# Gate table stored from ScalarE's queue, two more raw buffers and more gather steps in the U stage, a last V group of 4, and a halved id sum

## The chip, the cores and the metric

The kernel runs on one core of a Trainium2 chip. The metric is device time in microseconds (us), the median of several executions. PE is TensorE, DVE is VectorE, ACT is ScalarE, POOL is GpSimd, SP is the engine that issues most DMAs.

## The reference

One decoder layer over 16 meta tokens and 512 sequence tokens of width 2048: RMSNorm, differential attention and an mLSTM side by side, an output projection, and a PEER feed-forward. All in fp32. The change lies in the PEER part:

```
q = (ht @ w_q).reshape(T, 8, 2, 128)
s = einsum('thpd,hpnd->thpn', q, sub_keys)
s1, i1 = top_k(s[:, :, 0], 16);  s2, i2 = top_k(s[:, :, 1], 16)
cand_s = s1[..., :, None] + s2[..., None, :]
cand_i = i1[..., :, None] * 128 + i2[..., None, :]
best_s, best_pos = top_k(cand_s, 16)
idx = take_along_axis(cand_i, best_pos)          # 8 x 16 experts of 16384 for each token
gate = softmax(best_s)
act = gelu(einsum('td,tkd->tk', hb, u[idx]))
y = einsum('tk,tkd->td', gate * act, v[idx])
```

## The kernel before

**Dense and gathered tokens.** For ND = 352 tokens the kernel computes the PEER layer densely: all 16384 rows of `u` against these tokens (the U stage, 128 chunks of 128 experts), then all rows of `v` (the V stage), with a gate table that is zero where an expert was not chosen. The other 160 tokens are served by gathering: 128 of them in jobs "d" and "a", 32 (folded into 32 jobs "D" and "A") beside them. That makes NJ = 320 gather jobs, each an indirect DMA of 128 rows x 2048 floats (1.049 MB) issued by POOL at L836, and one DVE instruction that uses it (L844 with rows of `u`, L857 with rows of `v`). Three row buffers `ug` exist, so POOL is up to three gathers ahead of DVE. `run(n)` emits gather steps until n have been done.

**Order.** PE and DVE work in the order in which the program is written (a manual schedule), POOL too from the gate table on. ACT's and SP's queues are ordered by the scheduler of the framework, and each is served first in, first out.

**The routing stage (about 970 to 1160 us).** `step(n)` for n = 2 to 15 multiplies by `w_q` on PE while `bgstep()` runs the top-k in a pipeline of tasks: DVE max/index instructions, POOL's candidate grids `cd` (L935 to L939), the one-hot product `oh` on POOL (L969, 50 candidates x 16) and the DVE sum over the candidates `ids` (L974). A step does one `bgstep()`, every fourth step two, so 18 in these 14 steps; the other 16 fall among the first 31 U chunks.

**The U stage (about 1160 to 2262 us).** `u_chunk(c)` loads a chunk's weights in two halves of 128x1024 floats (512 KB each, `load_half` on SP's queue, three buffers `raw`), splits each into a high part (`hid`, ACT, L79) and a low part (`lod`, DVE, L80), which go into five buffers of each kind, and multiplies: 16 k-tiles x 3 matmuls of 352 columns (L89 to L91). The result goes through Gelu (`at`, L889) to the DRAM table `Ad` (L890, ACT's queue, 176 KB).

From chunk 32 on, the gate table is built beside it, four tokens at a time, 88 sets. `ebuild(q)` makes one-hot tiles on DVE (L1076 to L1079) and a scaled copy `ea` on ACT (L1081). The tiles `e` and `eg` are laid out as [128 keys, 4 tokens], so that one token's column has a step of four bf16 elements; `ea` is laid out densely. `gbuild(q)` is 12 matmuls of 128 columns (L1092), an ACT copy into the staging tile `stg` (L1093) and, every eighth set, the store of 2 MB to the DRAM table `Gd` from SP's queue (L1095). `stg` has one buffer.

`pace(c)` spreads the gather steps: from the 15 steps done before chunk 32 to JU = 150 at chunk 127. The last UTAIL = 6 chunks also hold the preparation of the first V group: loads of `Gd` and `Ad` (`p_load`, ACT's queue), the product `tm` (L1135) and its split into `ah` and `al` (L1145, L1146).

**The V stage (about 2262 to 3317 us).** Expert rows are handled in groups, GROUPS = [8] + [16] x 7 + [8] (sum 128). All groups but the last produce the transposed output (L1275 to L1277, 352 columns), 24 matmuls an item, an item being a 512 KB piece of `v` loaded as `rawv`; at the end of a group half, eight PSUM banks are added to `yT` on DVE (L1287). The last group (L1304 to L1306, 512 columns) runs token by token and ends with the final norm and the stores. Of six consecutive `rawv` loads three use the pool of the U stage, three a pool `vr` that lies on memory which the U stage holds until its end. In V, `run` spreads the remaining steps over all items but three of the transposed groups.

Of the kernel before, what the change touches and what calls it, by code (L numbers as in the profile page):

```python
# [8 lines left out]
F = mybir.dt.float32  # L9
R = mybir.dt.float32r  # L10
BF = mybir.dt.bfloat16
# [30 lines left out]
NQ = 128 // NB  # L42
SB = 128 // NQ
ND = S - 128 - NB
GROUPS = [8] + [16] * 7 + [8]
NJ = 2 * (128 + SB)
JU = 150
AR = 20
AR1 = 8

# [10 lines left out]
def body(tc, I, out):  # L61
    nc = tc.nc
    top = ExitStack()
    with top:
# [3 lines left out]
        dp = top.enter_context(tc.tile_pool(name="dp", bufs=1, space=DRAM))  # L68

        def load_half(src, name, rawp=None):  # L70
            raw = (rawp or wp).tile([128, 8, 128], F, name="raw" + name, tag="raw", bufs=3)
            nc.sync.dma_start(raw, src.rearrange("p (k c) -> p k c", k=8))
            return raw

        def split_half(src, name, raw=None, eng=nc.vector):
            raw = raw or load_half(src, name)
            hi = wp.tile([128, 8, 128], R, name="hi" + name, tag="whi")
            lo = wp.tile([128, 8, 128], R, name="lo" + name, tag="wlo")
            nc.scalar.copy(hi, raw)  # L79
            eng.tensor_tensor(lo, raw, hi.bitcast(F), op=OP.subtract)  # L80
            return hi, lo

        def split_tile(src, name):
            return [split_half(src[b], f"{name}_{b}") for b in range(2)]

        def mm3(ps, w, k, xh, xl, cs):
            hi, lo = w[k // 8]
# [578 lines left out]
def rest(tc, I, out, L):  # L666
# [150 lines left out]
    up = sU.enter_context(tc.tile_pool(name="up", bufs=1))  # L817
    iota = up.tile([128, 128], F, name="iota")
    nc.scalar.dma_start(iota, I["c_iota"])
    iota4 = up.tile([128, 128, 4], BF, name="iota4")  # L820
    nc.vector.tensor_copy(iota4, bcast(iota, 4))
    n1T = up.tile([128, ND], BF, name="n1T")
    n2T = up.tile([128, ND], BF, name="n2T")
    gp = up.tile([128, 3, ND], BF, name="gp")
# [46 lines left out]
    sp = [I["wq"][i] for i in range(16)] + [I["u"][c] for c in range(NK)]  # L871
    w[2] = split_tile(sp[2], "d2")

    def step(n, mid=None):
        if n + 1 < len(sp):
            w[n + 1] = split_tile(sp[n + 1], f"d{n + 1}")
        ps = pmu.tile([128, 512], F, name="pu", tag="pu")
        nn = S if n < 16 else ND
        for k in range(KD):
            mm3(ps[:, :nn], w[n], k, h2h, h2l, slice(0, nn))  # L880
            if k == 7 and mid:
                mid()
        w.pop(n)
        return ps
# [7 lines left out]
    with tc.tile_pool(name="tk", bufs=1) as tk, \  # L892
# [34 lines left out]
        def head_tasks(h, b):  # L927
            st = {}
            cs = slice(16 * h, 16 * h + 16)

            def grid(dst, lo, hi):
                o = 0
                for i in range(5):
                    n = 16 // (i + 1)
                    nc.gpsimd.tensor_tensor(dst[:, o:o + n], lo[:, :n], bcast(hi[:, i], n), op=OP.add)  # L935
                    o += n
                nc.gpsimd.tensor_tensor(dst[:, o:o + 6].rearrange("p (a c) -> p a c", c=2), bcast_mid(lo[:, :2], 3),
                                        bcast(hi[:, 5:8], 2), op=OP.add)
                nc.gpsimd.tensor_tensor(dst[:, o + 6:o + 14], hi[:, 8:16], bcast(lo[:, 0], 8), op=OP.add)  # L939

            bv = (gsel if b == 3 else gs[:, b])[:, cs]

            def t1():
                sv = tk.tile([128, 2, 16], F, name="sv", tag="sv", bufs=3)
                si = tk.tile([128, 2, 16], U32, name="si", tag="si", bufs=3)
                st["sv"], st["si"] = sv, si
                return [(sv[:, p, :], si[:, p, :], hd[h, p][:, b, :]) for p in range(2)]

            def t1b():
                sv, si = st["sv"], st["si"]  # L950
                cd = tk.tile([128, 2, NCAND], F, name="cd", tag="cd", bufs=4)
                sif = tk.tile([128, 2, 16], F, name="sif", tag="sif", bufs=3)
                nc.scalar.activation(sif[:, 0, :], si[:, 0, :], AF.Copy, scale=128.0)
                nc.scalar.copy(sif[:, 1, :], si[:, 1, :])
                grid(cd[:, 0, :], sv[:, 1, :], sv[:, 0, :])
                grid(cd[:, 1, :], sif[:, 1, :], sif[:, 0, :])
                st["cd"] = cd

            def t2():
                st["bp"] = tk.tile([128, 16], U32, name="bp", tag="bp", bufs=3)  # L960
                return [(bv, st["bp"], st["cd"][:, 0, :])]

            def t2b():
                bpb = tk.tile([128, 16], BF, name="bpb", tag="bpb", bufs=3)
                nc.vector.tensor_copy(bpb, st["bp"])
                eq = tk.tile([128, NCAND, 16], BF, name="eqb", tag="eqb", bufs=2)
                nc.vector.tensor_tensor(eq, iom, bcast_mid(bpb, NCAND), op=OP.is_equal)
                oh = tk.tile([128, NCAND, 16], F, name="oh", tag="oh", bufs=2)
                nc.gpsimd.tensor_tensor(oh, eq, bcast(st["cd"][:, 1, :], 16), op=OP.mult)  # L969
                st["oh"] = oh  # L970

            def t3():
                oh = st["oh"]
                nc.vector.tensor_reduce(ids[:, b, cs], oh.rearrange("p c k -> p k c"), axis=AX.X, op=OP.add)  # L974
                if b == 3:
                    nc.vector.tensor_copy(idx[:, cs], ids[:, 3, cs])
                    routed.append(h)
            return t1, t1b, t2, t2b, t3
# [84 lines left out]

    with tc.tile_pool(name="gk", bufs=1, reuse_waits="tile") as gk, \
            tc.tile_pool(name="psg", bufs=2, space=PSUM) as psg, \
            tc.manual_schedule(engines={mybir.EngineType.Pool}):
        stg = {}

        ge = {}

        def ebuild(q):
            t0 = 4 * q
            e = gk.tile([128, 2, 128, 4], BF, name="e", tag="e", bufs=2)
            eg = gk.tile([128, 2, 128, 4], BF, name="eg", tag="eg", bufs=2)
            ea = gk.tile([128, 4, 128], BF, name="ea", tag="ea", bufs=2)
            nc.vector.tensor_tensor(e[:, 0], iota4, bcast_mid(n1T[:, t0:t0 + 4], 128), op=OP.is_equal)  # L1076
            nc.vector.tensor_tensor(e[:, 1], iota4, bcast_mid(n2T[:, t0:t0 + 4], 128), op=OP.is_equal)
            for i in range(2):
                nc.vector.tensor_tensor(eg[:, i], e[:, 1], bcast_mid(gp[:, 1 + i, t0:t0 + 4], 128), op=OP.mult)  # L1079
            for j in range(4):  # L1080
                nc.scalar.activation(ea[:, j, :], e[:, 1, :, j], AF.Copy, scale=g0[:, t0 + j:t0 + j + 1])  # L1081
            ge[q] = e[:, 0], [ea.rearrange("p j n -> p n j"), eg[:, 0], eg[:, 1]]

        def gbuild(q):
            tg, r = divmod(4 * q, TG)
            if r == 0:
                stg[tg] = gk.tile([128, NK, TG], F, name="stg", tag="stg")
            e1, eg = ge.pop(q)
            pg = psg.tile([128, 4, 128], F, name="pg", tag="pg")
            for j in range(4):  # L1090
                for i in range(3):
                    nc.tensor.matmul(pg[:, j, :], e1[:, :, j], eg[i][:, :, j], start=(i == 0), stop=(i == 2))  # L1092
            nc.scalar.copy(stg[tg][:, :, r:r + 4], pg.rearrange("p j n -> p n j"))  # L1093
            if r + 4 == TG:
                nc.sync.dma_start(Gd[tg, :, 0:NK, :], stg[tg])  # L1095

        gr2.append(sG.enter_context(tc.tile_pool(name="gr2", bufs=1, side="right")))
        acc["D"] = gr2[0].tile([128, D], F, name="h2nB", tag="h2nB")
        for q in range(NQ):
            nc.scalar.dma_start(acc["D"][NB * q:NB * q + NB], hB)  # L1100
        ng, n0, c0 = 0, nj[1], ci
        ebuild(0)

        def pace(c):
            run(n0 + int((c + 1 - c0) * (JU - n0) / (NK - c0)))

        for c in range(ci, NK - UTAIL):
            u_chunk(c)
            while ng < min(ND // 4, (c + 1 - ci) * (ND // 4) / (NK - 12 - ci)):
                gbuild(ng)  # L1110
                ng += 1
                if ng < ND // 4:
                    ebuild(ng)
            pace(c)
    sU.close()

    with ExitStack() as sV:
# [40 lines left out]
        def vload(i):  # L1158
            if i < len(vord):
                g, dc, pr, c = vord[i]  # L1160
                vraw[i] = load_half(I["v"][g0s[g] // 2 + pr, dc if g == NG - 1 else 2 * dc + c], "v",
                                    None if i % 6 < 3 and i < nlast - 4 else vr[0])

        def vsplit(i):
            if i < len(vord):
# [27 lines left out]
        for c in range(NK - UTAIL, NK):  # L1193
            if c == NK - 1:
                for i in range(VLA):
                    vload(i)
                    vsplit(i)
            u_chunk(c)
            for _ in range(-(-len(pro) // (NK - c))):
                f, q = pro.pop(0)  # L1200
                f(q)
            pace(c)
        assert not pro
        sQ.close()
        sD.close()
# [258 lines left out]
```

## Time and profile before

| | |
|---|---|
| median of 3 executions | 3329.25 us (3327.45 to 3330.25) |
| the profiled execution | 3331.74 us |
| its span, first to last instruction | 3330.0 us |
| PE busy | 3264.0 us (98%) |
| DVE, ACT, POOL busy | 2320.2, 1325.5, 943.9 us |
| mean granted TensorE clock | 0.992 of full speed |
| moved by DMA | 815.47 MB, mean 245 GB/s |

Busy is the union of an engine's instructions. Matmuls overlap in the profile (a 352-column matmul is shown with some 325 ns but the next starts 160 ns after it), so PE's share alone does not say how close PE is to its rate; the number of matmuls in a stretch does.

### The profile page before, as it was taken

What the parts mean: (1) busy time and instruction counts of PE and PEld (TensorE: products, weight loads), DVE (VectorE), ACT (ScalarE), POOL (GpSimd) and SP (SyncE); (2) the same over time, 40 slices, a digit from 0 to 9 for tenths busy, and PEclk for the clock granted to TensorE, in tenths of its full rate; (3) what the DMA queues carried; (4) which work ended last, traced back from release to release, by engine and by line L of the source; (5) the groups of instructions that cost most, each with busy time, mean ns of one, the idle gap of its engine ahead of it and who ended that gap; (6) DMA issues with size and microseconds to landing.
All of it is one profiled execution on the core that took longest, in us unless ns stands there. A gap on an engine that the chain in (4) does not pass through costs nothing.

```text
span 3330.0 us, 51020 instructions
## 1 busy us (share of the span) xinstructions
PE 3264.0 (98%) x20126; PEld 3067.1 (92%) x20126; DVE 2320.2 (70%) x3504; ACT 1325.5 (40%) x2219; POOL 943.9 (28%) x942
## 2 busy tenths in 40 slices
PE   8999999999999999999999999997999999999998
PEld 7889898888887899999999999997999999999996
DVE  7444444444367788787877778767888888888973
ACT  5444444453252233444544544433333333333323
POOL 2011111110015566423332233322323323323312
PEclk8999999999999999999999999998999999999999
DMA  4222121123353266588888978999999999999972
GB/s 154 70 70 77 64 77 64 64 70 115 127 186 136 87 221 226 206 323 316 332 343 325 361 297 348 354 362 337 377 354 375 372 365 370 375 364 372 379 279 101
DMA packets 230162, 815.47 MB, mean 245 GB/s; under 512 B 21697, under 2 KB 85697, under 8 KB 186529
## 3 DMA queue, kind: packets, MB, share of 16 engines
q1 hardware_dynamic: 105488, 400.72, 33.3%
q0 software_dynamic: 46080, 335.56, 25.7%
q10 hardware_dynamic: 78352, 75.92, 6.8%
q8 instruction: 158, 2.59, 0.3%
q14 instruction: 84, 0.68, 0.1%
HBM read 757.33 MB, written 54.79 MB: 244 GB/s over the span
## 4 chain that ended last, share of the span: by engine, by line
PE 85%; DVE 8%; DMA 2%; issue 2%; ACT 1%; POOL 1%; ACTq 0%; SPq 0%; POOLq 0%; DVEq 0%
PE pu L89 10%; PE pu L90 10%; PE pu L91 10%; PE py L1275 8%; PE py L1277 8%; PE py L1276 8%; PE ps L89 5%; PE ps L91 5%; PE ps L90 5%; PE pg L1092 3%; PE po L742 2%; PE po L740 2%; PE po L741 2%; DVE y L857 1%; DVE lov L80 1%
## 5 line engine op out<-in xcount | busy, mean ns | idle before, releaser
L89 PE MATMUL pu<-hh,hid 128*128 128x352 f32 (+1 forms) x2272 | 759.8, 334 | 0.2 <-ACT at L889 0.2
L90 PE MATMUL pu<-hh,lod 128*128 128x352 f32 (+1 forms) x2272 | 751.3, 331 | 3.1 <-DVE lod L80 3.1
L91 PE MATMUL pu<-hl,hid 128*128 128x352 f32 (+1 forms) x2272 | 750.2, 330 | 0.0
L1275 PE MATMUL py<-ah,hiv 128*128 128x352 f32 x1920 | 627.0, 327 | 20.5 <-ACT hiv L79 9.5
L1276 PE MATMUL py<-ah,lov 128*128 128x352 f32 x1920 | 623.4, 325 | 8.8 <-DVE lov L80 8.8
L1277 PE MATMUL py<-al,hiv 128*128 128x352 f32 x1920 | 625.5, 326 | 0.0
L79 ACT CAST hiv<-rawv 128x1024 fp32r<-128x1024 f32 x256 | 269.2, 1053 | 572.4 <-PE py L1277 462.6
L80 DVE TENSOR_TENSOR lod<-rawd,hid 128x1024 fp32r<-128x1024 f32 x284 | 361.0, 1287 | 176.7 <-ACT hid L79 175.5
L90 PEld LDWEIGHTS pu<-hh,lod 128*128 128x128 f32 x2272 | 428.2, 188 | 12.8 <-DVE lod L80 3.4
L89 PEld LDWEIGHTS pu<-hh,hid 128*128 128x128 f32 x2272 | 429.9, 189 | 10.3 <-ACT at L889 0.8
L91 PEld LDWEIGHTS pu<-hl,hid 128*128 128x128 f32 x2272 | 428.1, 188 | 9.7
L79 ACT CAST hid<-rawd 128x1024 fp32r<-128x1024 f32 x284 | 297.8, 1050 | 347.2 <-DMA rawd<-in_u_dram 235.1
L89 PE MATMUL ps<-xh,hiz 128*128 128x256 f32 (+2 forms) x1280 | 410.9, 321 | 1.3 <-DVE qT L369 1.2
L836 POOL DMA_INDIRECT ug<-in_un_dram,idx x128 | 249.2, 1947 | 522.3 <-DVE ug L844 500.8
L91 PE MATMUL ps<-xl,hiz 128*128 128x256 f32 (+2 forms) x1280 | 392.8, 307 | 0.0
L90 PE MATMUL ps<-xh,loz 128*128 128x256 f32 (+2 forms) x1280 | 392.5, 307 | 0.0
L1275 PEld LDWEIGHTS py<-ah,hiv 128*128 128x128 f32 x1920 | 363.0, 189 | 24.2 <-issue 12.9
L1276 PEld LDWEIGHTS py<-ah,lov 128*128 128x128 f32 x1920 | 362.6, 189 | 11.8 <-DVE lov L80 11.8
L836 POOL DMA_INDIRECT ug<-in_vn_dram,idx x128 | 229.0, 1789 | 469.7 <-DVE y L857 444.3
L1277 PEld LDWEIGHTS py<-al,hiv 128*128 128x128 f32 x1920 | 361.9, 188 | 0.0
L80 DVE TENSOR_TENSOR lov<-rawv,hiv 128x1024 fp32r<-128x1024 f32 x256 | 313.4, 1237 | 33.7 <-ACT hiv L79 33.5
L857 DVE SCALAR_TENSOR_TENSOR y<-ug,act,y 128x2048 f32<-128x2048 f32 x127 | 298.3, 2349 | 14.8 <-DMA ug<-in_vn_dram,idx 14.8
(342 smaller groups left out, 5029.9 us busy)
## 6 DMA issues: line engine op xcount, KB each, us to landing
rawd<-in_u_dram SPq DMA_DIRECT2D x256, 512.0 KB
rawv<-in_v_dram SPq DMA_DIRECT2D x256, 512.0 KB
rawz<-in_wz_dram SPq DMA_DIRECT2D x98, 512.0 KB
Ad<-at ACTq DMA_DIRECT2D x128, 176.0 KB
Gd<-stg SPq DMA_DIRECT2D x11, 2048.0 KB
gt<-Gd ACTq DMA_DIRECT2D x32, 704.0 KB
av<-Ad ACTq DMA_DIRECT2D x64, 352.0 KB
rawwo<-in_wo_dram SPq DMA_DIRECT2D x40, 512.0 KB
```

What stands on the lines that cost most here:

```text
L79: nc.scalar.copy(hi, raw)
L80: eng.tensor_tensor(lo, raw, hi.bitcast(F), op=OP.subtract)
L89: nc.tensor.matmul(ps, a, xh[k][:, cs], start=(k == 0), stop=False)
L90: nc.tensor.matmul(ps, b, xh[k][:, cs], start=False, stop=False)
L91: nc.tensor.matmul(ps, a, xl[k][:, cs], start=False, stop=(k == KD - 1))
L740: nc.tensor.matmul(ps[tb], mh[n][:, sl], h, start=(n == 0), stop=False)
L836: nc.gpsimd.indirect_dma_start(out=t, out_offset=None, in_=I["un" if kind in "dD" else "vn"], in_offset=bass.IndirectOffsetOnAxis(ap=ix[:, ...
L857: nc.vector.scalar_tensor_tensor(acc[kind], t, o, acc[kind], op0=OP.mult, op1=OP.add)
L1092: nc.tensor.matmul(pg[:, j, :], e1[:, :, j], eg[i][:, :, j], start=(i == 0), stop=(i == 2))
L1275: nc.tensor.matmul(po, h, ah, start=(pr + j == 0), stop=False)
L1276: nc.tensor.matmul(po, l, ah, start=False, stop=False)
L1277: nc.tensor.matmul(po, h, al, start=False, stop=(2 * pr + j == n - 1))
```

## The change

- `Gd` is stored from ACT's queue instead of SP's, and the copy of a set out of PSUM is taken out of `gbuild` into `gcopy`, which the loop calls before the next set's matmuls, one chunk later. Because of that the sets are spread over five chunks fewer (NK - 17 instead of NK - 12), the last at chunk 110 instead of 115.
- The one-hot tiles are laid out as two pairs, [2, 128 keys, 2 tokens], so that one token's column has a step of two elements instead of four. `iota4` becomes `iota2`, built by two copies.
- From chunk 32 to 121, every second and fourth of five U loads goes to a pool `ru` of two buffers, so five raw buffers in all.
- JU goes from 150 to 174, and `pace` reaches it at chunk 121: 159 steps in 90 chunks (1.767 a chunk) where there were 135 in 96 (1.406 a chunk). The six tail chunks emit no gather steps.
- GROUPS ends in [4, 4] instead of [8].
- After `oh`, POOL adds the second half of the candidates to the first, and DVE's sum `ids` reads 25 x 16 elements instead of 50 x 16.

```
-GROUPS = [8] + [16] * 7 + [8]
+GROUPS = [8] + [16] * 7 + [4, 4]
-JU = 150
+JU = 174
...
         def load_half(src, name, rawp=None):
-            raw = (rawp or wp).tile([128, 8, 128], F, name="raw" + name, tag="raw", bufs=3)
+            pool, n = rawp or (wp, 3)
+            raw = pool.tile([128, 8, 128], F, name="raw" + name, tag="raw", bufs=n)
...
-    iota4 = up.tile([128, 128, 4], BF, name="iota4")
-    nc.vector.tensor_copy(iota4, bcast(iota, 4))
+    iota2 = up.tile([128, 2, 128, 2], BF, name="iota2")
+    for i in range(2):
+        nc.vector.tensor_copy(iota2[:, i], bcast(iota, 2))
...
+    def uload(n):
+        if n < len(sp) and n not in w:
+            ps = [None, None]
+            if ru:
+                for b in range(2):
+                    if ru[1] % 5 in (1, 3):
+                        ps[b] = (ru[0], 2)
+                    ru[1] += 1
+            w[n] = split_tile(sp[n], f"d{n}", ps)
...
                 nc.gpsimd.tensor_tensor(oh, eq, bcast(st["cd"][:, 1, :], 16), op=OP.mult)
-                st["oh"] = oh
+                nc.gpsimd.tensor_tensor(oh[:, 0:NCAND // 2], oh[:, 0:NCAND // 2], oh[:, NCAND // 2:], op=OP.add)
+                st["oh"] = oh[:, 0:NCAND // 2]
...
+        def pairs(t):
+            a = [list(p) for p in t.ap]
+            return bass.AP(tensor=t.tensor, offset=t.offset, ap=[a[0], [2 * a[1][0], 2], [0, 128], [a[1][0], 2]])
...
-            e = gk.tile([128, 2, 128, 4], BF, name="e", tag="e", bufs=2)
+            e = gk.tile([128, 2, 2, 128, 2], BF, name="e", tag="e", bufs=2)
...
-            nc.vector.tensor_tensor(e[:, 0], iota4, bcast_mid(n1T[:, t0:t0 + 4], 128), op=OP.is_equal)
+            nc.vector.tensor_tensor(e[:, 0], iota2, pairs(n1T[:, t0:t0 + 4]), op=OP.is_equal)
...
-                    nc.tensor.matmul(pg[:, j, :], e1[:, :, j], eg[i][:, :, j], start=(i == 0), stop=(i == 2))
-            nc.scalar.copy(stg[tg][:, :, r:r + 4], pg.rearrange("p j n -> p n j"))
-            if r + 4 == TG:
-                nc.sync.dma_start(Gd[tg, :, 0:NK, :], stg[tg])
+                    nc.tensor.matmul(pg[:, j, :], e1[:, j // 2, :, j % 2], eg[i][:, j // 2, :, j % 2],
+                                     start=(i == 0), stop=(i == 2))
+            gd[q] = pg
+
+        def gcopy(q):
+            tg, r = divmod(4 * q, TG)
+            if r == 0:
+                stg[tg] = gk.tile([128, NK, TG], F, name="stg", tag="stg")
+            nc.scalar.copy(stg[tg][:, :, r:r + 4], gd.pop(q).rearrange("p j n -> p n j"))
+            if r + 4 == TG:
+                nc.scalar.dma_start(Gd[tg, :, 0:NK, :], stg[tg])
...
-            run(n0 + int((c + 1 - c0) * (JU - n0) / (NK - c0)))
+            run(n0 + int((c + 1 - c0) * (JU - n0) / (NK - UTAIL - c0)))
 
         for c in range(ci, NK - UTAIL):
             u_chunk(c)
-            while ng < min(ND // 4, (c + 1 - ci) * (ND // 4) / (NK - 12 - ci)):
+            while ng < min(ND // 4, (c + 1 - ci) * (ND // 4) / (NK - 17 - ci)):
+                if ng - 1 in gd:
+                    gcopy(ng - 1)
                 gbuild(ng)
                 ng += 1
                 if ng < ND // 4:
                     ebuild(ng)
+            if ng == ND // 4 and gd:
+                gcopy(ng - 1)
             pace(c)
+        ru.clear()
...
                 f, q = pro.pop(0)
                 f(q)
-            pace(c)
```

## Rows read from the trace of the kernel before

**Rows 1.** The page, busy time: engine, us, share of the span, instructions.

```profile
PE 3264.0 (98%) x20126; PEld 3067.1 (92%) x20126; DVE 2320.2 (70%) x3504; ACT 1325.5 (40%) x2219; POOL 943.9 (28%) x942
```

**Rows 2.** Windows: us, busy PE PEld DVE ACT POOL (instructions), clock, DMA share, GB/s.

```profile
1420.00:2164.00 744.00, 743.43 (x5039) 731.39 (x5037) 586.57 (x755) 361.96 (x689) 235.12 (x118) 1.00 0.87 334
2164.00:2224.00 60.00, 60.00 (x377) 60.00 (x376) 35.09 (x34) 17.03 (x22) 15.34 (x9) 1.00 0.98 375
2224.00:2264.00 40.00, 34.74 (x203) 33.63 (x201) 29.25 (x36) 14.79 (x22) 12.81 (x6) 0.96 0.88 329
2264.00:2370.00 106.00, 89.93 (x502) 86.65 (x503) 77.88 (x89) 38.17 (x62) 28.82 (x18) 0.92 0.94 349
2370.00:3100.00 730.00, 720.89 (x4436) 718.28 (x4435) 636.91 (x591) 236.60 (x278) 237.44 (x133) 1.00 0.97 369
```

**Rows 3.** Waits of PE, whole run: us in total, times, longest us.

```profile
PE py L1275 <- ACT hiv L79: 9.5, 3, 7.2
PE py L1275 <- DVE yT L1287: 8.9, 10, 1.0
PE py L1276 <- DVE lov L80: 8.8, 9, 2.2
PE pscore L919 <- ACT qt L982: 7.7, 4, 3.4
```

**Rows 4.** Timeline of PE through two gate sets in a row: start, us, instruction.

```profile
1608.35 0.25 PE L1092 MATMUL pg<-ea,e 128*128 128x128 bf16 x1
1608.44 0.40 PE L1092 MATMUL pg<-eg,e 128*128 128x128 bf16 x2
1608.65 0.24 PE L1092 MATMUL pg<-ea,e 128*128 128x128 bf16 x1
...
1610.63 0.41 PE L89 MATMUL pu<-hh,hid 128*128 128x352 f32 x1
```

**Rows 5.** Groups by form, 1417 to 2164 us: busy us, mean ns, idle before.

```profile
L844 DVE SCALAR_TENSOR_TENSOR ug<-ug,h2n 128x2048 f32<-128x2048 f32 x113 | 256.0, 2286 | 1.3 <-DMA ug<-in_un_dram,idx 1.3
L80 DVE TENSOR_TENSOR lod<-rawd,hid 128x1024 fp32r<-128x1024 f32 x170 | 204.7, 1222 | 91.6 <-ACT hid L79 90.8 <-issue 0.7
...
L1079 DVE TENSOR_TENSOR eg<-e,gp 128x512 bf16<-128x512 bf16 x176 | 67.0, 422 | 3.0
L1093 ACT COPY stg<-pg 128x512 f32<-128x512 f32 x87 | 50.7, 583 | 35.1 <-DMA Gd<-stg 32.0 <-PE pg L1092 2.4 <-ACT at L889 0.8
```

**Rows 6.** Source L844 up to 1417 us: count, duration ns min/median/max.

```profile
L844 DVE SCALAR_TENSOR_TENSOR ug<-ug,h2n x15: 2277/2279/2284, 1168.9 to 1386.1; 128x2048 f32<-128x2048 f32 x15
```

**Rows 7.** Timeline of SP at the start of V: start, us.

```profile
2261.04 0.97 SPq L1221 DMA_DIRECT2D xr<-x1d  x1
2269.63 15.03 SPq L72 DMA_DIRECT2D rawv<-in_v_dram  x5
```

**Rows 8.** Timeline of ACT at the same place, with the idle time before it.

```profile
2282.00 1.05 ACT L79 CAST hiv<-rawv 128x1024 fp32r<-128x1024 f32 x1 [10.03 <-DMA rawv<-in_v_dram]
```

**Rows 9.** Source L974, the id sums: durations, and what DVE waited for.

```profile
L974 DVE TENSOR_REDUCE ids<-oh x32: 1520/1541/1550, 1000.1 to 1393.9; 128x16 f32<-128x800 f32 x32
...
  POOL oh L969: 20.1, 9
```

**Rows 10.** Groups of POOL by form, whole run.

```profile
L371 POOL TENSOR_TENSOR qT<-qT,sw 128x512 f32<-128x512 f32 x8 | 12.5, 1559 | 4.0 <-DVE qT L369 3.5
...
L485 POOL TENSOR_TENSOR o<-o,ssq 128x512 f32<-128x512 f32 x8 | 8.5, 1057 | 0.6
```

**Rows 11.** Timeline of PE in the last group, first and last of 22 matmuls.

```profile
3298.66 0.40 PE L1306 MATMUL py<-hiv,al 128*128 128x512 f32 x1
...
3303.57 0.39 PE L1306 MATMUL py<-hiv,al 128*128 128x512 f32 x1
```

**Rows 12.** The page, DMA issues: queue, count, KB each.

```profile
Gd<-stg SPq DMA_DIRECT2D x11, 2048.0 KB
```

## Prediction before the run

> **What bounds the kernel now.** I read the busy times first: PE is busy for 98% of the span [rows 1], so time can only be won where PE works less, or where it stands. The windows by stage say where that is [rows 2]. The reader should look at the matmul counts, for they show the rate. From 2164 to 2224 us PE does nothing but U matmuls, 377 in 60 us, or 0.159 us each, 7.63 us for a chunk's 48. From 1420 to 2164 us it does 5039, of which 88 x 12 = 1056 belong to the gate table; the other 3983 cost 633 us, so the 88 sets cost 111 us, 1.26 us each. PE is never short of work there (743.43 of 744 us busy). In steady V (2370 to 3100 us) it does 4436 in 720.89 us, 0.1625 us each.
>
> Between the two it falls behind. From 2224 to 2264 us 203 matmuls at 0.159 us need 32.3 of 40 us: 7.7 us lost. From 2264 to 2370 us 502 at 0.1625 us need 81.6 of 106 us: 24.4 us lost, the granted clock down to 0.92 of the window (stretches at 1.2 instead of 2.4 GHz after PE had stood), which is in the count. So 32 us go at the passage from U to V, and this is the largest loss in the changed part. The list of PE's waits gives the rest: split V weights (9.5 and 8.8 us, nearly all in this passage), the `yT` sums at group ends (8.9 us), and `qt` in the routing stage (7.7 us) [rows 3].
>
> What is late at the passage is the weight loads. SP's queue puts out a blocked group of `rawv` loads only from 2269.63 us [rows 7], and ACT waits 10.03 us for the next to land [rows 8]. The DMA is full there, and DVE, in program order, does gather steps of 2286 ns [rows 5] ahead of the subtraction that frees the raw buffer for which SP's first load waits.
>
> **The change, part by part.** My sum is made against the profiled execution, 3331.74 us, whose span is 3330.0; it lies 2.5 us over the median of 3329.25.
>
> *Gather steps.* 15 steps lie before chunk 32 [rows 6]. Bytes for a chunk: two weight halves 1.049 MB, `at` 0.180 MB, 2.097 MB of `Gd` for eight sets [rows 12], 1.049 MB a gather. Before, with 1.406 gathers and 88/84 sets a chunk, this is 2.98 MB in 7.63 + 1.05 x 1.26 = 8.95 us, 333 GB/s; the window shows 334 [rows 2], so the account holds. After, with 1.767 gathers and 88/79 sets, it is 3.37 MB for each of the 79 chunks 32 to 110, and 3.08 MB for the 11 chunks to 121: 300 MB. The rate at full share: 375/0.98 = 383, 334/0.87 = 384, 369/0.97 = 380 GB/s [rows 2]. I take 383: 784 us for the 90 chunks.
>
> *The gate layout.* `ea` is dense and `eg` has a step of four elements. The `eg` after an `ea` starts 0.09 us later, the two `eg` take 0.21 us together until the next `ea`, and the 24 matmuls of two sets take 2.28 us [rows 4]. If a step of two reads as densely as `ea`, eight matmuls of a set gain 0.02 us each: 0.16 us a set, 14 us for 88. Bounds: nothing (the step costs the same), and the pace of 0.159 us for 352 columns [rows 2], which would be 0.058 us for 128, so 0.5 us a set and 46 us. I take the nearest row, `ea`, which differs in one operand only. PE alone then needs 90 x 7.63 + 88 x 1.10 = 784 us for these chunks, as long as the DMA; before it was 798 us. With both at their limit I allow 0.9% for waits and take 791: 7 us won.
>
> The Trainium skill (SBUF — State Buffer, section Door 1) says that SBUF is read in lines of 16 bytes and that bf16 can be read at steps up to 8 elements without loss. By that, the step of four was free and the layout gives PE nothing; the rows speak against it, for `eg` does follow more slowly than `ea` [rows 4].
>
> *DVE in these chunks.* Two splits of 1222 ns, 1.114 sets of four 422 ns instructions and 1.767 steps of 2286 ns [rows 5] are 2.44 + 1.88 + 4.04 = 8.4 us at most in a chunk of 8.8; consecutive instructions overlap a little, and in steady V DVE is at 637 of 730 us without holding PE up much [rows 2]. The pair layout keeps 512 elements an instruction: I take 422 ns; at 690 ns DVE would need 9.6 us and bind.
>
> *Store, copies and raw buffers.* The store's issue moves behind ACT's copies. What it frees is SP: loads no longer stand behind a store that waits for ACT. PE does not wait there before [rows 2], so its price is nothing; the cover is the loads of two more raw buffers and the five split halves, about two chunks of work. If it is gone, what shows is ACT's wait for the one `stg` buffer, 32.0 us in all before [rows 5], with Gelu and the casts behind it; that wait may grow, since the store now shares the DMA with the loads instead of taking its turn among them. The copies lie off PE's path. The end of the sets at chunk 110 leaves 12 chunks before the first read of `Gd`.
>
> *The passage.* Before, the six tail chunks (46 us of matmuls) had to move 6.3 MB of U weights, 1.1 of `at`, 4.3 of `Gd` and `Ad` for the first V group, 1.6 of V weights and 9.4 for nine gathers: 22.7 MB, 59 us at 383 GB/s. After, no gather steps are there but the three rows that POOL has already asked for: 16.4 MB, 43 us, which fits. DVE loses 9 x 2.29 = 21 us of steps that stood ahead of its splits, so SP's first load is freed early. What stays: PE's 2 us wait for the last Gelu, the loads into memory that U holds to its end, and some low clock; I keep 9 of the 32 us. Won: 23. Bounds: 5 (the late loads stay) to 30.
>
> *The rest of V.* 146 steps instead of 170, 0.596 instead of 0.717 an item. DVE has 55 us more room; of the 8.9 us at group ends I take 1. V's DMA falls from 369 to about 350 GB/s.
>
> *Last groups.* Four rows of experts move from the direct to the transposed form. Direct: 22 matmuls from 3298.66 to 3303.57 us, 0.234 us each [rows 11]; 36 a row, 8.4 us. Transposed: 48 x 0.1625 = 7.8 us. So 2.5 us won and one more group end at 2 x 0.9 us lost [rows 3]; and in the last third of the output each token block has 2.8 us of matmuls where it had 5.6, so that the norm of one shows behind the next: 1 us. Together 0.
>
> *Id sums.* A sum takes 1541 ns and DVE waited 20.1 us for `oh` [rows 9], so POOL's add lies in the chain of a routing step. 400 elements at 1057 or 1559 ns for 512 [rows 10] are 0.83 to 1.22 us, I take 1.0; the halved sum is between 0.77 and 1.0, I take 0.85. Net 0.3 us longer, 18 times, 5 us; PE feels it only in the steps with two tasks, where it waits for `qt` (7.7 us). I add 4; bounds 0 to 12. The second `iota2` copy is under this.
>
> Sum: -7 (chunks 32 to 121) - 23 (passage) - 1 + 0 + 4 = -27; 3331.74 - 27 = 3305, and 2.5 less for the median: **3302 us**.
>
> **The rivals.**
>
> *The DMA can't carry U (the other side).* The gathers moved out of V and the tail need 300 MB in the 90 chunks. The rest of the sum wins 20 us, so the change turns to a loss when these chunks take 818 us, at 367 GB/s; by 0.2%, at 364. V's mean is 369 [rows 2], with share 0.97, and U's last 60 us had 375, so it is near. At 360 GB/s, 833 us: +35 - 20, so 3344 us. The Trainium skill (DMA: Bandwidth & Descriptors, section Where 436 GB/s comes from) has about 358 GB/s as the limit between HBM and one core; by that figure U takes 838 us and the time is 3349. The windows of 369 and 375 GB/s are above it, so I don't follow it. Chance 0.14.
>
> *The layout gives PE nothing,* and U stays at 798 us with its DMA at 376 GB/s: 7 us less won, 3309 us. For it: the weights `e` keep a step. Chance 0.24.
>
> *The layout gives more and the DMA carries it:* 300 MB at 390 GB/s is 770 us, 21 us more won than I sum: 3281 us. Chance 0.15.
>
> *The passage stays.* The loads into memory of the U stage start only when PE leaves it, gathers or not; then 5 instead of 23 us are won: 3320 us. For it: the group of loads at 2269.63 us [rows 7]; against it: DVE's gather steps in front of the first of them. Chance 0.13.
>
> **How the numbers follow.** My forecast has 0.34. What a measurement of this kernel can tell from no change is about 0.2%, 6.7 us: from 3322.6 to 3335.9. My case, both layout rivals and most of the passage rival lie below: 0.34 + 0.24 + 0.15 + 0.08 = 0.81; the rest of the passage rival and the mild part of the DMA rival within: 0.08; slower 0.11. The range leaves out what is over 3326 (0.13) and a little at the low end: 3283 to 3326.
>
> **What would show it.** Right, if the windows of the changed profile have 370 to 385 GB/s over chunks 32 to 121 and PE still busy, sets of about 1.1 us, and some 9 us lost around the start of V, with no 10 us wait of ACT for `rawv`. Wrong, if PE waits for `lod` or `hid` in the middle of U, if a gate set still takes 1.26 us, if ACT's wait for the `Gd` store is several times 32 us, or if `qt` waits well over 12 us.

## The result, and the profile after

The changed kernel takes 3288.38 us (3284.91 to 3289.89) beside 3329.0 us for the kernel before: a ratio of 0.9876, 95% interval 0.9863 to 0.9888, or 41 us less. The forecast was 3302 us, with a range of 3283 to 3326. The profiled execution has a span of 3288.1 us where the one before had 3330.0, so its difference of 41.9 us can be laid out by stage. For that I cut both traces at the same matmuls: the last 6144 matmuls of U are 128 chunks of 48, and V's are counted from its first. The windows of the kernel before, cut so, are chunks 32 to 121, the tail of six chunks, the first 768 matmuls of V, and the next 4992 (columns as in [rows 2]):

```profile
1411.80:2210.10 798.30, 797.73 (x5379) 785.55 (x5378) 619.09 (x787) 380.78 (x717) 247.18 (x126) 1.00 0.87 334
2210.10:2264.05 53.95, 48.64 (x289) 47.53 (x288) 36.58 (x43) 18.68 (x27) 16.09 (x8) 0.97 0.91 345
2264.05:2413.10 149.05, 133.03 (x768) 129.75 (x769) 115.15 (x119) 50.53 (x74) 45.11 (x26) 0.94 0.96 360
2413.10:3236.50 823.40, 812.12 (x4995) 808.98 (x4994) 712.82 (x659) 264.22 (x308) 257.64 (x144) 1.00 0.96 363
```

The same four stretches of the changed kernel, and last a part of the first:

```profile
1412.20:2204.30 792.10, 770.25 (x5379) 757.42 (x5378) 686.04 (x839) 371.92 (x718) 297.83 (x157) 0.98 0.97 378
2204.30:2256.00 51.70, 48.46 (x290) 47.87 (x288) 26.26 (x32) 17.45 (x27) 5.10 (x3) 0.97 0.91 314
2256.00:2388.00 132.00, 126.22 (x769) 124.08 (x770) 101.61 (x95) 50.44 (x73) 34.16 (x20) 1.00 0.92 345
2388.00:3197.20 809.20, 809.20 (x4993) 809.20 (x4992) 660.61 (x629) 262.50 (x304) 200.58 (x124) 1.00 0.90 338
...
2117.00:2204.00 87.00, 84.99 (x526) 84.69 (x525) 69.17 (x51) 27.56 (x34) 25.96 (x19) 1.00 1.02 414
```

So 6.2 us came from chunks 32 to 121, 2.3 from the tail, 17.1 from the start of V, 14.2 from the rest of V, and the last group with the end gave 2.6; up to chunk 32 nothing moved (+0.4). Together 42. The reader should also see what the first line hides: PE is now idle 21.8 of 792 us there, with the granted clock down to 0.98; before, it was idle for 0.6 us. PE's list of waits, against [rows 3]:

```profile
PE pu L91 <- DVE lod L81: 16.6, 6, 5.5
PE pscore L932 <- ACT qt L996: 10.1, 4, 3.9
PE py L1305 <- DVE lov L81: 5.8, 6, 1.7
PE pg L1110 <- ACT ea L1101: 5.1, 3, 3.0
PE pu L90 <- ACT at L902: 2.7, 1, 2.7
```

The waits for `hiv` and for `yT` are gone; a wait for `lod` in the middle of U, which the prediction named as a sign against itself, has come. The gate sets, beside [rows 4]: from one `ea` to the next it is now 0.18 us instead of 0.30.

```profile
1617.54 0.23 PE L1110 MATMUL pg<-ea,e 128*128 128x128 bf16 x1
1617.61 0.28 PE L1110 MATMUL pg<-eg,e 128*128 128x128 bf16 x2
1617.72 0.22 PE L1110 MATMUL pg<-ea,e 128*128 128x128 bf16 x1
```

One place where PE stands for `lod` shows how. ACT issues a store of the gate table at 1663.66 us and at its next copy waits for it (idle time and releaser in brackets; first the timeline of ACT, then of POOL, DVE and PE):

```profile
1663.66 0.33 ACTq L1120 DMA_DIRECT2D Gd<-stg  x1
...
1679.87 0.58 ACT L1118 COPY stg<-pg 128x512 f32<-128x512 f32 x1 [8.06 <-DMA Gd<-stg]
1680.35 2.13 ACT L80 CAST hid<-rawd 128x1024 fp32r<-128x1024 f32 x2
```

```profile
1664.36 2.75 POOL L838 DMA_INDIRECT ug<-in_un_dram,idx  x1 [3.13 <-DVE ug L846]
```

```profile
1680.35 2.29 DVE L846 SCALAR_TENSOR_TENSOR ug<-ug,h2n 128x2048 f32<-128x2048 f32 x1 [6.26 <-DMA ug<-in_un_dram,idx]
...
1682.57 2.36 DVE L81 TENSOR_TENSOR lod<-rawd,hid 128x1024 fp32r<-128x1024 f32 x2
```

```profile
1683.84 0.66 PE L91 MATMUL pu<-hh,lod 128*128 128x352 f32 x1 [5.52 <-DVE lod L81]
```

The gather issued just after the store lands 16 us later (from 1420 to 2204 us a gather takes 7.0 us at least, 9.8 in the median, 17.0 at most). DVE stands 6.26 us at the step that uses it, and the split that PE needs is behind that step in DVE's program order. Behind ACT's wait of 8.06 us for `stg` stand two casts, and the split needs the first of them, which ends at about 1681.4 us: without the late gather PE would have stood here some 1.2 us less. So the store holds PE in two ways at this place.

### The profile page after: what moved, and what is told of

Same layout as the page of the kernel before. It is cut to its first block, busy times and chain, and to the rows that moved or that the text cites. A ratio compares the mean times of both kernels' runs of the same rounds, so it can differ in the third digit from the quotient of the medians.

```text
span 3288.1 us, 51152 instructions
## 1 busy us (share of the span) xinstructions
PE 3222.9 (98%) x20174; PEld 3038.4 (92%) x20174; DVE 2323.8 (71%) x3521; ACT 1315.1 (40%) x2219; POOL 932.0 (28%) x974
## 4 chain that ended last, share of the span: by engine, by line
PE 64%; issue 18%; POOL 10%; DVE 4%; DMA 3%; ACT 1%; ACTq 0%; POOLq 0%; SPq 0%; DVEq 0%
PE py L1304 9%; PE py L1306 9%; PE py L1305 9%; POOL ug L838 8%; PE ps L90 6%; PE ps L92 5%; PE ps L91 5%; PE pu L90 3%; PE pu L91 3%; PE pu L92 3%; PE po L743 2%; PE po L741 2%; PE po L742 2%; DMA ug<-in_vn_dram,idxB 1%; PE pn L534 1%
## 5 line engine op out<-in xcount | busy, mean ns | idle before, releaser
L91 PE MATMUL pu<-hh,lod 128*128 128x352 f32 (+1 forms) x2272 | 756.2, 333 | 16.7 <-DVE lod L81 16.6
L1305 PE MATMUL py<-ah,lov 128*128 128x352 f32 x1984 | 641.4, 323 | 5.8 <-DVE lov L81 5.8
L1304 PE MATMUL py<-ah,hiv 128*128 128x352 f32 x1984 | 644.4, 325 | 0.6 <-ACT at L902 0.6
L1306 PE MATMUL py<-al,hiv 128*128 128x352 f32 x1984 | 643.8, 325 | 0.0
L838 POOL DMA_INDIRECT ug<-in_vn_dram,idx x128 | 208.3, 1627 | 618.6 <-DVE y L859 598.2
L1305 PEld LDWEIGHTS py<-ah,lov 128*128 128x128 f32 x1984 | 372.7, 188 | 7.9 <-DVE lov L81 7.9
L1304 PEld LDWEIGHTS py<-ah,hiv 128*128 128x128 f32 x1984 | 372.8, 188 | 0.8 <-ACT at L902 0.8
L1306 PEld LDWEIGHTS py<-al,hiv 128*128 128x128 f32 x1984 | 372.0, 187 | 0.0
L846 DVE SCALAR_TENSOR_TENSOR ug<-ug,h2n 128x2048 f32<-128x2048 f32 x128 | 304.2, 2396 | 39.3 <-DMA ug<-in_un_dram,idx 39.0
```

Of the source, the lines that this page charges most:

```text
L91: nc.tensor.matmul(ps, b, xh[k][:, cs], start=False, stop=False)
L838: nc.gpsimd.indirect_dma_start(out=t, out_offset=None, in_=I["un" if kind in "dD" else "vn"], in_offset=bass.IndirectOffsetOnAxis(ap=ix[:, ...
L846: nc.vector.scalar_tensor_tensor(t, t, 1.0, acc[kind], op0=OP.mult, op1=OP.mult, accum_out=o)
L1304: nc.tensor.matmul(po, h, ah, start=(pr + j == 0), stop=False)
L1305: nc.tensor.matmul(po, l, ah, start=False, stop=False)
L1306: nc.tensor.matmul(po, h, al, start=False, stop=(2 * pr + j == n - 1))
```

## The experiments

Where the time went in every run, cut as above (us; chunks 32 to 121 with PE's idle time and the DMA's GB/s in them; "V, first" are its first 768 matmuls, "V, rest" the next 4992):

| run | median | chunks 32 to 121 | idle | GB/s | tail | V, first | V, rest |
|---|---|---|---|---|---|---|---|
| before | 3329 | 798.3 | 0.6 | 334 | 54.0 | 149.1 | 823.3 |
| changed | 3288.4 | 792.1 | 21.8 | 378 | 51.7 | 132.0 | 809.3 |
| a1_old_layout | 3303.3 | 809.7 | 8.1 | 370 | 49.1 | 131.7 | 809.3 |
| a2_old_pace | 3272.9 | 760.1 | 2.1 | 353 | 50.2 | 143.3 | 812.6 |
| a3_store_sp | 3279.3 | 780.7 | 16.5 | 383 | 53.9 | 131.6 | 809.3 |
| a4_old_groups | 3288.4 | 789.8 | 22.2 | 379 | 52.0 | 131.7 | 809.3 |
| b1_layout_only | 3308.4 | 772.4 | 10.3 | 345 | 55.0 | 148.3 | 822.9 |
| b2_pace_only | 3336.0 | 843.0 | 27.2 | 356 | 51.3 | 132.3 | 809.3 |
| b3_old_ids | 3284.6 | 788.8 | 20.8 | 380 | 49.4 | 132.9 | 809.3 |
| b4_three_raw | 3330.3 | 827.3 | 47.7 | 362 | 50.6 | 131.8 | 809.3 |
| c1_clean_tail | 3258.6 | 761.6 | 2.1 | 364 | 46.8 | 130.9 | 812.6 |
| c2_combined | 3254.4 | 760.5 | 2.5 | 365 | 46.8 | 130.9 | 812.6 |
| c3_combined_162 | 3255.1 | 765.2 | 6.7 | 377 | 47.3 | 132.6 | 809.6 |
| c4_weights_only | 3326.8 | 796.3 | 0.6 | 335 | 54.6 | 148.0 | 823.2 |

**a1_old_layout**: the changed kernel with the old gate tiles.

```
-            e = gk.tile([128, 2, 2, 128, 2], BF, ...)      (eg, ea, iota2 likewise)
+            e = gk.tile([128, 2, 128, 4], BF, ...)
```

> The changed kernel with the gate tiles in the old layout (a step of four). Theory: the layout is why a set of gate matmuls costs PE about 0.93 us instead of 1.26 us in the changed profile, so PE alone needs 29 us more for the 90 chunks 32 to 121; but most of the 26 us that PE stands there waiting for the low halves goes away, since PE is then slower than the DMA. Chunks 32 to 121 take 798 to 806 us instead of 792, the whole 3294 to 3302 us, and a set costs 1.26 us. First rival: the step of the layout costs PE nothing and the sets are cheaper for another reason: 3288 us, set 0.93 us. Second rival: the waits for the low halves stay whole, because they come from bursts of the DMA and not from a mean rate: 3317 us.

Measured 3303.33 us, ratio to before 0.9931 (0.9917 to 0.9944): 15 us more than changed, all in chunks 32 to 121 (809.7 us), and PE's idle time falls from 21.8 to 8.1 us. The theory holds, some us above its upper end: part of what the layout gives PE goes back as waits.

**a2_old_pace**: the changed kernel with the old spread of gather steps.

```
-JU = 174
+JU = 150
...
-            run(n0 + int((c + 1 - c0) * (JU - n0) / (NK - UTAIL - c0)))
+            run(n0 + int((c + 1 - c0) * (JU - n0) / (NK - c0)))
...
                 f(q)
+            pace(c)
```

> The changed kernel with the old spread of gather steps: 150 by chunk 127, the tail chunks included. Theory: the steps taken out of V are what removed 17 us at its start and 12 to 15 us at its group ends, and the steps put into U are what makes PE wait 26 us there. Then V takes some 30 us more, chunks 32 to 121 some 20 us less (about 770 us), the tail 2 us more: 3298 to 3304 us. Rival: the waits at the group ends went for another reason (they stay away here): 3284 to 3290 us. Second rival: the waits in U come from the store of the gate table alone, whatever the number of gathers, and stay: 3318 us.

Measured 3272.88 us, ratio 0.983 (0.9816 to 0.9845): 15.5 us *less* than the changed kernel. My theory had the gain in V at twice its size (V takes 14.6 us more here, not 30) and the loss in U too small (32.0 us, not 20). Moving the steps costs more than it brings in the kernel as changed. The first three stretches of this run:

```profile
1415.00:2175.10 760.10, 758.00 (x5380) 747.04 (x5379) 619.01 (x788) 370.46 (x717) 242.44 (x126) 1.00 0.91 353
2175.10:2225.30 50.20, 46.53 (x290) 45.95 (x289) 34.98 (x41) 17.76 (x26) 14.48 (x7) 0.99 0.94 344
2225.30:2368.60 143.30, 130.66 (x769) 128.10 (x770) 113.11 (x116) 51.06 (x74) 42.16 (x26) 0.97 0.96 366
```

With 1.4 steps a chunk in place of 1.77 PE has nearly no idle time in the first, at full clock.

**a3_store_sp**: the changed kernel with the store on SP's queue.

```
-                nc.scalar.dma_start(Gd[tg, :, 0:NK, :], stg[tg])
+                nc.sync.dma_start(Gd[tg, :, 0:NK, :], stg[tg])
```

> The changed kernel with the store of the gate table issued from SP's queue again, the copies one chunk later as changed. Theory: on ScalarE's queue the 2 MB store runs beside the loads and the gathers; gathers then land 15 to 17 us after their issue instead of 9, DVE stands at a gather step with the splits behind it, and PE waits for the low halves at 7 of the 11 stores. From SP's queue the loads stand still during a store and the gathers do not: waits of PE in U fall from 26 to under 12 us, time 3270 to 3280 us. Rival: the bytes set it, not the queue: 3285 to 3291 us. Second rival: the loads stand behind the store, and with PE faster now the split halves run out: over 3295 us.

Measured 3279.32 us, ratio 0.9849 (0.9834 to 0.9863): 9 us less, chunks 32 to 121 in 780.7 us. PE's wait for `lod`:

```profile
PE pu L91 <- DVE lod L81: 9.3, 4, 4.8
```

The time lies in the theory's range, and this wait fell from 16.6 to 9.3 us. The store's queue is a cause, but with it undone most of the idle time stays (16.5 us, where the theory had under 12), so it isn't the only one. The theory's mechanism, that the gathers land sooner, is not shown: from 1410 to 2205 us DVE stands at gather steps for some 62 us here and for some 67 us in the changed kernel.

**a4_old_groups**: `GROUPS` ends in [8] again.

> The changed kernel with one last group of 8 rows instead of two of 4. By the sum on record the edit is worth nothing (2.5 us won, 2.8 us lost): 3288 us. By the changed profile, whose group ends cost no time, only the 2.5 us are left: 3290 to 3291 us. Rival: the shorter last group also shortens the end behind the last matmul: over 3293 us.

Measured 3288.37 us, ratio 0.9879 (0.9863 to 0.9894): nothing that can be told from the changed kernel, as the sum had it. But the trace shows more than the median. Behind V's first 5760 matmuls this run takes 93.5 us to its end, as every run with [8] does, and every run with [4, 4] takes 90.9. So the edit gives 2.6 us, as the second expectation said; here chunks 32 to 121 were 2.3 us shorter and hid it.

**b1_layout_only**: the kernel before with the pair layout alone (the lines of the change's diff from `iota4` to the matmuls of L1092).

> The kernel before with the pair layout of the gate tiles alone. By the term on record (0.16 us a set, 88 sets): 14 us less, 3315 us, a set at 1.10 us. By the changed profile (0.33 us a set): 29 us less, 3300 us, a set at 0.93 us, the DMA at some 347 GB/s beside it. Rival: the layout alone gives nothing: 3329 us.

Measured 3308.35 us, ratio 0.9939 (0.9924 to 0.9953). Chunks 32 to 121:

```profile
1411.60:2184.10 772.50, 762.23 (x5380) 749.77 (x5379) 615.23 (x785) 373.54 (x717) 245.41 (x125) 1.00 0.90 345
```

PE is busy for 762.23 us where it was for 797.73, so the layout takes 35 us off PE's work, more than either expectation; 10.3 us come back as idle time, most of it behind ACT, which from 1410 to 2205 us waits 289.0 us for `rawd` here. Chunks 32 to 121 gain 25.9 us, nearer to the second expectation than to the term on record; the median, 21 us less, lies between the two.

**b2_pace_only**: the kernel before with the change's spread of gather steps (the three places of a2, the other way round).

> The kernel before with the changed spread of gather steps alone (174 by chunk 121, none in the tail). Theory: 20 us are won around the start of V and 12 to 15 us at the group ends, as in the changed kernel; PE, at 798 us for chunks 32 to 121, loses up to 10 us there to the DMA: 3294 to 3304 us. Rival: the group ends need the other edits as well: 3306 to 3312 us. Second rival: without the two more raw buffers and with the store on SP's queue the DMA cannot carry the steps, and chunks 32 to 121 lose 25 us or more: over 3318 us.

Measured 3336.02 us, ratio 1.0023 (1.0013 to 1.0032): 0.2% slower. Both the theory and the second rival are half right. V gains all that the changed kernel gains there, and chunks 32 to 121 lose 44.7 us:

```profile
1409.20:2252.20 843.00, 815.82 (x5379) 799.60 (x5377) 685.03 (x838) 376.36 (x717) 311.24 (x157) 0.98 0.92 356
...
2303.50:2435.90 132.40, 127.37 (x769) 125.23 (x770) 103.23 (x98) 50.49 (x73) 35.99 (x20) 0.99 0.93 348
2435.90:3245.10 809.20, 809.20 (x4993) 809.20 (x4992) 668.28 (x638) 264.22 (x308) 207.71 (x123) 1.00 0.91 342
```

**b3_old_ids**: the id sums wholly on DVE again.

```
-                nc.gpsimd.tensor_tensor(oh[:, 0:NCAND // 2], oh[:, 0:NCAND // 2], oh[:, NCAND // 2:], op=OP.add)
-                st["oh"] = oh[:, 0:NCAND // 2]
+                st["oh"] = oh
```

> The changed kernel with the id sums wholly on DVE again. By the sum on record: 4 us less, 3284 us, with PE's wait for qt back from 10.1 to 7.7 us. Rival: the routing stage is bound elsewhere and the edit is worth nothing: 3288 us.

Measured 3284.56 us, ratio 0.9872 (0.9854 to 0.989): 4 us less, as on record, though the intervals overlap. The routing stage itself is clearer: from its first to its last `pscore` matmul PE takes 178.5 us before, 182.3 changed, 176.9 here.

**b4_three_raw**: the changed kernel without the pool `ru`.

```
-        ru += [rup, 0]
```

> The changed kernel with three raw buffers in U. By the sum on record the two more buffers are worth nothing, and the waits in U come from DVE standing at gather steps, not from loads that start late: 3286 to 3291 us. Rival: the loads of the two more buffers are what carries PE over a store of the gate table: 10 us or more lost in chunks 32 to 121, over 3298 us.

Measured 3330.3 us, ratio 1.0007 (0.9999 to 1.0016). The rival was right: without the two buffers the whole gain is gone. Chunks 32 to 121:

```profile
1413.00:2240.30 827.30, 779.58 (x5380) 761.96 (x5377) 685.18 (x838) 373.49 (x717) 304.19 (x157) 0.97 0.93 362
```

Waits from 1410 to 2205 us, of this run:

```profile
ACT hid L80 <- DMA rawd<-in_u_dram: 275.1, 132, 6.2
...
PE pg L1109 <- ACT ea L1100: 26.4, 11, 9.2
```

and of the changed kernel, from 1410 to 2205 us too:

```profile
ACT hid L80 <- DMA rawd<-in_u_dram: 72.9, 39, 7.7
```

With three buffers a load can only start when a split has freed its buffer, ACT stands at the cast until it lands, and the `ea` copies and Gelu for which PE waits are behind the cast on ACT. The sum of ACT's wait is not the price: b1_layout_only has 289.0 us of it and 10.3 us of idle time. What is behind it counts, and what comes together. Before PE's longest wait here ACT stood first for the store and then for a load:

```profile
1495.87 0.58 ACT L1117 COPY stg<-pg 128x512 f32<-128x512 f32 x1 [9.46 <-DMA Gd<-stg]
...
1498.76 1.04 ACT L80 CAST hid<-rawd 128x1024 fp32r<-128x1024 f32 x1 [1.36 <-DMA rawd<-in_u_dram]
1499.71 1.28 ACT L1100 ACTIVATE ea<-e,g 128x128 bf16<-128x128 bf16 x4
```

```profile
1500.16 0.27 PE L1109 MATMUL pg<-ea,e 128*128 128x128 bf16 x1 [9.17 <-ACT ea L1100]
```

**c1_clean_tail**: the changed kernel with `JU = 150`, its `pace` kept (150 by chunk 121, none in the tail).

> The changed kernel with JU = 150, still reached at chunk 121 and with no steps in the tail: 1.5 steps a chunk. Theory: with 150 steps by chunk 127 the chunks 32 to 121 took 760 us, bound by PE, and the start of V 11 us more than in the changed kernel, because steps of the tail and of V stand on DVE ahead of the splits; the tail's share of that goes here, and 1.5 instead of 1.4 steps a chunk cost PE under 5 us: 3258 to 3268 us, the first 768 matmuls of V in some 132 us. Rival: it is the number of steps left for V, and not the tail, that holds up its start: 3270 to 3276 us, first 768 matmuls in 143 us.

Measured 3258.56 us, ratio 0.9796 (0.9783 to 0.981). The theory holds. V has 170 steps left as in a2_old_pace, and still its start takes 130.9 instead of 143.3 us. SP's queue shows why; first a2_old_pace, then this run:

```profile
2222.19 0.65 SPq L1251 DMA_DIRECT2D xr<-x1d  x1
2230.48 29.20 SPq L73 DMA_DIRECT2D rawv<-in_v_dram  x8
```

```profile
2219.30 0.33 SPq L1250 DMA_DIRECT2D xr<-x1d  x1
2220.27 37.09 SPq L73 DMA_DIRECT2D rawv<-in_v_dram  x10
```

With steps in the tail the next group of V's loads starts 8.3 us behind the load of `xr`, as in [rows 7]; without them it is 1 us. DVE in a2_old_pace, just before 2230.48 us:

```profile
2224.77 2.29 DVE L846 SCALAR_TENSOR_TENSOR ug<-ug,h2nB 128x2048 f32<-128x2048 f32 x1
...
2226.98 2.29 DVE L846 SCALAR_TENSOR_TENSOR ug<-ug,h2nB 128x2048 f32<-128x2048 f32 x1
...
2229.20 1.22 DVE L81 TENSOR_TENSOR lov<-rawv,hiv 128x1024 fp32r<-128x1024 f32 x1
```

The group starts as this split ends. So it was DVE's steps ahead of the splits that held up the loads, not memory that U holds. The tail's DMA is also spared most of its gathers in c1; what share of the gain that has was not separated.

**c2_combined**: c1_clean_tail with the store on SP's queue (a3) and the old id sums (b3).

> The kernel c1_clean_tail with the store of the gate table on SP's queue and the id sums wholly on DVE. Theory: the id sums give 4 us; the store's queue gives nothing where the DMA has room (it gave 9 us where DVE stood at gather steps): 4 us under c1_clean_tail. Rival: on SP's queue the loads wait behind the store and the raw buffers run out: as long as c1_clean_tail, or more.

Measured 3254.39 us, ratio 0.9786 (0.9773 to 0.9799): the lowest median of all, about 1% under the changed kernel and 4.2 us under c1, whose interval it overlaps. Chunks 32 to 121 don't move (760.5 us): where PE is the limit, the store's queue is free. ACT still waits 48.8 us for `stg` from 1410 to 2205 us, but PE is idle for only 2.5 us in these chunks.

**c3_combined_162**: c2_combined with `JU = 162`.

> The kernel c2_combined with JU = 162, 1.63 steps a chunk. Theory: the steps of U cost where the landing of a gather and not PE sets the pace; 174 cost 32 us in chunks 32 to 121 against 150, and about half of the range lies under the bend, so 162 takes some 765 to 772 us there and saves 4 us in V: within 6 us of c2_combined, more likely above. Rival: the DMA carries 284 MB at 378 GB/s in 751 us, less than PE's 758, so U loses nothing and V gains: 4 us under c2_combined.

Measured 3255.12 us, ratio 0.9792 (0.9779 to 0.9806), the same as c2: 4.7 us more in chunks 32 to 121, 3.0 less in the rest of V. PE begins to stand between 150 and 162 steps (6.7 us idle, after 2.5).

**c4_weights_only**: the kernel before, with the pair layout for the weights alone.

```
-            e = gk.tile([128, 2, 128, 4], BF, name="e", tag="e", bufs=2)
+            e = gk.tile([128, 2, 128, 2], BF, name="e", tag="e", bufs=2)       (weights, step of two)
+            e2 = gk.tile([128, 128, 4], BF, name="e2", tag="e2", bufs=2)       (for eg and ea, step of four)
...
-                    nc.tensor.matmul(pg[:, j, :], e1[:, :, j], eg[i][:, :, j], ...)
+                    nc.tensor.matmul(pg[:, j, :], e1[:, j // 2, :, j % 2], eg[i][:, :, j], ...)
```

> The kernel before with the pair layout for the one-hot tile that PE loads as weights alone; the moving tiles keep their step of four. By the reading on record (the dense ea against eg shows the price of the moving operand's step; the weights' step is free): starts after ea 0.08 us apart and after eg 0.10 us, as before, and 3329 us. By the run with the layout alone (both kinds fell to 0.06 us, the dense ea too, whose only change was its weights): after ea 0.058 us, after eg 0.06 to 0.08 us, and 3308 to 3318 us.

Measured 3326.76 us, ratio 1.0003 (0.9994 to 1.0012): no gain. From one `ea` to the next it is again 0.28 to 0.29 us:

```profile
1603.29 0.23 PE L1100 MATMUL pg<-ea,e 128*128 128x128 bf16 x1
1603.35 0.39 PE L1100 MATMUL pg<-eg,e 128*128 128x128 bf16 x2
1603.57 0.24 PE L1100 MATMUL pg<-ea,e 128*128 128x128 bf16 x1
...
1603.86 0.24 PE L1100 MATMUL pg<-ea,e 128*128 128x128 bf16 x1
```

It is the moving operand's step of four that costs. With the moving `eg` at a step of two, all starts are 0.06 us apart (changed kernel); with it at four, the two `eg` of a token take 0.22 us together.

## Why the prediction was right, and where its steps were not

The time came out inside the range, 14 us under the forecast, and 13 of these lie in the rest of V. Of the working, the sizes of the passage and the routing stand; the account of chunks 32 to 121 gave the right number from wrong parts.

- **Chunks 32 to 121**: forecast 798 to 791 us, measured 798.3 to 792.1. That these agree is luck. PE's work alone is 758.00 us there (the a2 row) and not 784, so the layout gave 26 us more than forecast; waits and a lower clock took 34 us where I had allowed 7, and the two errors cancel. The DMA's 784 us was nearer: a3 needed 781 with the same steps. But 383 GB/s is no single limit. The same 300 MB took 792 us as changed, 827 without the new buffers and 843 with the kernel before's layout, store and buffers, and the changed kernel's last 87 us in these chunks ran at 414 GB/s.
- **The layout**: forecast 0.16 us a set. PE's busy time fell from 797.73 to 758.00 us, 39.7 us or 0.45 us a set, close to the upper bound (0.5); the layout alone took 35.5 us off it (b1). DVE's instructions for the pairs stayed at 422 ns, as assumed. The failed reading is that of `ea` as the price of a dense operand. `ea` is dense in both kernels, and yet the next matmul started 0.078 us after it before and starts 0.058 us after it now (means over the 352 of each). So such a distance is not the price of one operand; the sum over the three matmuls of a token (0.30 us, then 0.18) prices the step. The rival that the layout gives nothing falls; that it gives more was right on PE's side. The Trainium skill (SBUF — State Buffer, section Door 1) has bf16 steps of up to 8 elements as free; for the moving operand of these matmuls the runs show the contrary, 0.45 us a set between a step of four and one of two. For the weights it agrees: c4 moved PE's stretch by 2 us.
- **Gather steps in U**: taken as carried by a DMA with room up to 383 GB/s. The change's spread cost 32.0 us there (760.1 to 792.1), more than the 14.6 us that it brings in V; c1 has 135 steps in these chunks at 761.6 us, so 24 more than those cost 30. With PE's work at 758 us, the forecast's own rate would have put 26 us on them, so that rate alone is not what failed. What a mean rate misses shows in c3: its 288 MB at 383 GB/s need 753 us, less than PE's 758, and still PE is idle for 6.7 us. PE stands when one gather, or one load, lands late and the split it needs is queued behind the wait for it, as at 1683.84 us. The DMA's share is 0.97 over the changed kernel's 792 us; how much of the lateness is a DMA that is simply full was not tested.
- **The raw buffers**: priced at nothing, and named only as cover for the store. They are worth 35 us in these chunks (827.3 against 792.1), and without them the rival that the DMA can't carry U came true: b4_three_raw shows 362 GB/s, and b2_pace_only, which lacks the layout and the store's new queue too, 356 GB/s and 3336 us, where that rival had 3344 us at 360. That is close to the figure of about 358 GB/s between HBM and one core in the Trainium skill (DMA: Bandwidth & Descriptors, section Where 436 GB/s comes from), but it is no limit here: the changed kernel moved 378 GB/s over the 792 us, and 414 from 2117 to 2204 us.
- **The store**: priced at nothing, with ACT's wait for `stg` expected to grow from 32.0 us. It grew to 47.8 us, and the queue costs 9 to 11 us (a3), but only beside 174 steps (c2).
- **The passage**: forecast 23 us, measured 19.4 (tail and first 768 matmuls of V, 203.1 to 183.7). c1 confirms the mechanism, and shows that an empty tail does it without more steps in U: 177.7 us. In the changed kernel ACT's longest wait for `rawv` at this place is 2.8 us in place of 10.0 [rows 8]. The rival that the passage stays falls.
- **The rest of V**: the term that was off most, 1 us forecast and 14 measured. The waits for `yT` at the group ends went with the steps (b2_pace_only: 809.3 us as well): before, DVE did a step of 2.35 us and splits ahead of the `yT` adds, and with 24 fewer steps it is there in time. That a2 and c1, with as many steps in V as before, have 812.6 and not 823.3 us must come from another edit; there PE waits for `yT` 1.9 and 1.7 us, with b1's layout alone still 8.9. The last groups are the only other edit that touches V: they make its transposed part 248 items instead of 240, so that 170 steps are 0.694 an item instead of 0.717. But [4, 4] with 170 steps against [8] with 170 was not tried by itself.
- **Last groups**: forecast 0 as 2.5 us won and 2.8 lost, measured 2.6 won in the traces (93.5 to 90.9 us at the end of V). The loss at one more group end did not come. In a4's median the gain can't be seen.
- **Id sums**: forecast 4 us lost, measured 3.8 in the routing stage (178.5 to 182.3), 5.4 against the changed kernel without the edit (b3). It is hidden in the total, for the stretch before the first `pscore` matmul, whose code did not change, was 3.4 us shorter in the profile after. That is the spread between executions: in the fourteen profiles this stretch ends between 982.4 and 987.8 us.

In sum, -6.2 for -7, -19.4 for -23, -14 for -1, -2.6 for 0, and +0.4 for +4.

## What to carry to other kernels

A transfer stage is not described by bytes over one rate alone: ask which engine, in program order, stands at which landing, and what is queued behind it; two buffers more were worth 35 us and one queue 9, at the same bytes. Work should be moved to another stage only as far as the new place has slack in each engine's order: 135 steps in these chunks cost PE next to nothing, 159 cost more than they bring, and the gain at the passage came from where the steps are (none in the tail), not from how many go into U. Undo each part of a change by itself once it is measured as a gain; here the changed kernel hid 34 us (3288.4 to 3254.4).

## What the runs showed that I had not expected

A moving bf16 operand with a step of four elements takes about twice the time of one with a step of two: with 128 columns, the starts were 0.056 us apart at two and 0.10 at four, means over some 700 `eg` matmuls of each kernel, while the same step in the weights changed little. And a wait of PE costs more than its idle time. In chunks 32 to 121 the changed kernel has 21.8 us of idle time, but its busy time too is 12 us above a2_old_pace's (770.25 and 758.00 us for the same matmuls), at a granted clock of 0.98 for the stretch, a mixture of stretches at 2.4 GHz with some at 1.2 GHz after PE had stood (0.50 from 1683.00 to 1689.50 us, behind the wait of 5.52 us).
